# RWKV-7 recurrence in a two-layer decoder: order of values, transposes and final norms, and buffers of the sample states

## Chip, cores, metric

The kernel runs on one core of one Trainium2 chip. The metric is the device time of one execution in microseconds (us): 2224.28 us before the change, the median of three runs (2219.95 to 2230.23). The engines are named TensorE (PE; its weight loads PEld), VectorE (DVE), ScalarE (ACT), GpSimd (POOL) and SyncE (SP, which issues the DMAs here).

## The reference

One inference step of a trunk with two layers, in float32, width 1024. A prompt of 1024 rows with 16 learned rows ahead of it, and 8 samples of 8 rows each, go through the same weights: 1104 rows in all. Layer 0 is a gated DeltaNet. Layer 1 is RWKV-7 with 16 heads of width 64; the change touches only its recurrence, what stands around it, and the final norm. Cut to that:

```python
def rwkv_mixer(xn, S0, shift_prev, ...):
    r, k, v, z = ...                       # four projections of the token-shifted input
    decay = jnp.exp(-jnp.exp(w)); b_h = kk * a_h
    def step(S, inp):
        S = S * d_t + (S @ -kk_t) outer b_t + v_t outer k_t
        return S, S @ r_t                  # per head, 64 x 64 state
    S, y = lax.scan(step, S0, ...)
    y = (y - mean) * lax.rsqrt(var + GN_EPS) * lnx_w + lnx_b      # group norm per head
    y = y + jnp.sum(r_h * k_h * r_k, -1, keepdims=True) * v_h     # "bonus"
    y = y.reshape(B, T, D) * jax.nn.silu(z)
    return y @ w_o, S, xn[:, -1]
...
x = x + out
y = rmsnorm(x, final_norm_w)               # after the last layer
```

The outputs are the normed rows of the prompt and of the samples, and the states of both layers for both.

## The kernel before

The rows lie on the free axis, in three segments of 384, 384 and 336 (the first holds the 64 sample rows, chunk 0). The scan is done in chunks of 64 rows in matrix form. An *item* n = 8 s + p is one pair of heads p in one segment s: 24 items of 6 chunks each. The function `wave` runs them in *turns*: item n starts at turn T = 2 n and does one chunk a turn, so three items are in flight in each turn, and two turns start one new item. The turns run from -2 to 51, with a tail after them.

One turn on TensorE: `step_solve` (xX and rA from the state rS and AR), half of an item's *scores* (fG), `step_inner` (rA from X and rTT), `step_values` (xX of the next turn from UV and G), `step_state` (rA from UV with BT and G), and then the *dense part*: matmuls that don't hang on the recurrence, the gates (zz) till turn 14, then the output projection of segments 0, 1 and 2 (zo, at the end fo). The chain through a turn: xX goes to X on ScalarE, X through TensorE to UV on ScalarE, UV through TensorE to rS on VectorE and y on ScalarE, and rS to the next turn's xX.

All other work of an item is put at a turn, a phase of it (0 ahead of `step_solve`; 1 behind it; 1.5, 2 and 3 behind `step_state`, where 2 and 3 share the dense part between them) and a number that sorts it within the phase: `put(turn, phase, function, number)`. Each engine works through its own queue in the order in which the program is written; nothing is reordered later. The pieces that the text speaks of, by tile:

- load: DMAs of fldcs, fldr, fldv, BK, AR, rTT for an item. exps: fDp on ScalarE and DC on GpSimd. reads: AR on VectorE. pair and halves: pr on VectorE, prh on ScalarE, prl on GpSimd.
- bonus: two matmuls fbonus from prh and prl, then rbv on VectorE. values: three transposes fVT, then two copies to UV on ScalarE.
- stats and `rwkv_finish`: group norm of y (batch-norm statistics and a root on VectorE, grs on GpSimd, the scaling of y on GpSimd, for the items 22 and 23 on ScalarE with gnb), the transposes of y (dyT), their evacuation t, the gate, and the split in two float32r halves yh (ScalarE) and yl (GpSimd).
- `rwkv_sample_read`: for the 8 items of segment 0 the sample states are loaded (sn, four DMAs), transposed (dsn), copied to Sb and read. `rwkv_sample_write` brings them back (sso).
- `project_out` streams the weights of the output projection: wraw (two buffers), whi by a cast on ScalarE, wlo by a subtraction on GpSimd, as everywhere in this kernel.
- `finish(s)`: the final norm of a segment in three tiles of 128 rows: transposes (dfin, ffin, rfin), a square with a sum on ScalarE into f2k, a product with the weight on VectorE (L2073), the sum fr and its root frs, a scaling of f2k (GpSimd in the segments 0 and 1, VectorE in segment 2) and the output DMA from f2k. `fill` hands out its steps evenly over turns 31 to 45 (segment 0) and 47 to 51.5 (segment 1).

PSUM tiles have a bank by their first letter: "d" has one buffer, "f" two, "z" one, "r" three, "x" one. A new tile waits till the one before it in the same buffer has been read.

Of the kernel before, what the change touches and what calls it, by code (L numbers as in the profile page):

```python
# [11 lines left out]
ALU = mybir.AluOpType  # L12
# [13 lines left out]
class Gaps:  # L26
# [3 lines left out]
    def put(self, g, f, prio=2):  # L30
        self.q.setdefault(max(g, self.now), []).append((prio, f))
# [57 lines left out]
class Builder:  # L89
# [1604 lines left out]
    def rwkv_item(self, n, put):  # L1694

        nc, t, col = self.nc, self.t, self.pcol
        P = Ctx()
# [3 lines left out]
        T = 2 * n  # L1701
# [217 lines left out]
    def rwkv_finish(self, P, a, b):  # L1919
# [13 lines left out]
        if P.n > 21:  # L1933
            nb = t(ap, [128, 6], "gnb", 1)[:, 0:m]
            nc.vector.scalar_tensor_tensor(nb, mv[:, a:b, 0], -1.0, rs, op0=ALU.mult, op1=ALU.mult)
        for q in range(a, b):
            if P.n > 21:
                self.act(y[:, q], y[:, q], AF.Identity, scale=P.rs[:, q:q + 1], bias=nb[:, q - a:q - a + 1])
            else:
                nc.gpsimd.tensor_scalar(y[:, q], y[:, q], mv[:, q, 0:1], P.rs[:, q:q + 1], op0=ALU.subtract, op1=ALU.mult)  # L1940
# [23 lines left out]
    def rwkv_sample_read(self, P):  # L1964
# [13 lines left out]
        nc.scalar.copy(P.Sb.rearrange("p b k -> p (b k)"), sp)
# [76 lines left out]
    def finish(self, s, x2):  # L2055
# [3 lines left out]
        for q in range(3):  # L2059
# [24 lines left out]
            for h in (0, 1):  # L2084
                hs = slice(512 * h, 512 * h + 512)
                v = y[h]
                if s < 2:
                    nc.gpsimd.tensor_scalar(v[0:nr], v[0:nr], rs[0:nr], None, op0=ALU.mult)
                else:
                    nc.vector.scalar_tensor_tensor(v[0:nr], ps[h][0:nr], rs[0:nr], self.fw[0:nr, hs], op0=ALU.mult, op1=ALU.mult)  # L2090
# [436 lines left out]
    def wave(self, zin, stay, last, pool):  # L2527
# [127 lines left out]
```

## Time and profile before

| what | value |
|---|---|
| device time, median of three runs | 2224.28 us |
| profiled execution | 2241.65 us |
| its span, first to last instruction | 2239.9 us |
| mean granted clock of TensorE | 0.972 of full speed |
| busy TensorE | 2093.9 us, 93% of the span |
| busy VectorE | 1430.2 us, 64% |
| busy ScalarE | 1261.5 us, 56% |
| busy GpSimd | 1261.8 us, 56% |

The recurrence runs from about 1800 us to the end. A row of the timeline has the start, the duration, the engine, the line, the operation with output and inputs, shapes and the count of instructions that were drawn together; in brackets behind it stands how long the engine had waited before the row and for which instruction. A group of waits has three numbers: us in all, times, the longest. A row of a window has the busy time of each engine, with the count of instructions, the granted clock (1.00 is full speed), and the DMA engines' share.

### The profile page before, as it was taken

The page shows a single profiled execution, that of the slowest core. Times are in us where ns is not written, and L with a number is a line of the kernel's source. Part 1 is how long each engine was busy: PE and PEld are TensorE (multiplying, and loading weights), DVE is VectorE, ACT ScalarE, POOL GpSimd, SP SyncE. Part 2 cuts the span into 40 slices and gives each one's busy share as a digit, 9 for nine tenths or more (in the row PEclk, how much of TensorE's full clock was granted, in tenths as well). Part 3 has the DMA queues.
Part 4 walks back from the last instruction along what each step waited for, and adds up shares of the span by engine and source line. Part 5 has one row for each costly group of instructions (what it writes and reads, how often), then busy time and mean ns, then how long its engine had stood idle before and what let it go on. Part 6 is the DMA issues. An engine that isn't in the chain of part 4 may idle for free. (4 is left out here: it accounts for less than half of the span.)

```text
span 2239.9 us, 56232 instructions
## 1 busy us (share of the span) xinstructions
PE 2093.9 (93%) x20958; PEld 1955.0 (87%) x20958; DVE 1430.2 (64%) x3638; ACT 1261.5 (56%) x3627; POOL 1261.8 (56%) x1902
## 2 busy tenths in 40 slices
PE   8889999999999999989999999998989988998886
PEld 7879989899999989878998999998989977887876
DVE  7857585766757585975435762768647246776654
ACT  5526565556656565645433564756546456776653
POOL 3417768585858585525241451347668636676674
PEclk9989999999999999999999999999999989999997
DMA  4324242424343332436254235586885566755532
GB/s 119 85 58 125 65 125 73 108 80 114 86 116 95 98 108 75 131 79 177 89 148 100 68 111 173 190 253 186 239 231 146 152 172 163 200 160 153 159 116 80
DMA packets 510763, 291.67 MB, mean 130 GB/s; under 512 B 240777, under 2 KB 495866, under 8 KB 510490
## 3 DMA queue, kind: packets, MB, share of 16 engines
q1 hardware_dynamic: 510490, 288.08, 46.2%
q8 instruction: 166, 2.72, 0.5%
q14 instruction: 107, 0.88, 0.1%
HBM read 195.66 MB, written 92.30 MB: 129 GB/s over the span
## 5 line engine op out<-in xcount | busy, mean ns | idle before, releaser
L143 POOL TENSOR_TENSOR wlo<-wraw,whi 128x512 fp32r<-128x512 f32 x190 | 250.1, 1318 | 238.1 <-ACT whi L139 211.3
L692 POOL TENSOR_TENSOR invT<-invT,invtmp 72x31 f32<-72x31 f32 (+36 forms) x341 | 214.4, 629 | 26.7
L634 DVE SCALAR_TENSOR_TENSOR cvy<-raw,cw,cvy 128x408 f32<-128x408 f32 (+2 forms) x288 | 200.4, 696 | 34.2 <-ACT cvy L115 30.3
L690 POOL TENSOR_TENSOR invtmp<-invA,invT 72x31 f32<-72x31 f32 (+36 forms) x341 | 204.2, 599 | 24.8 <-DMA invA<-rltd 5.0
L129 PE MATMUL d<-xc,whi 128*128 128x384 f32 (+1 forms) x640 | 177.0, 342 | 0.0
L139 ACT CAST whi<-wraw 128x512 fp32r<-128x512 f32 x238 | 146.0, 615 | 24.4 <-DMA wraw<-in_rwkv_w_rkvz 8.5
L129 PE MATMUL dv<-xc,whi 128*128 128x384 f32 (+1 forms) x480 | 154.3, 342 | 0.0
L129 PE MATMUL dz<-xc,whi 128*128 128x384 f32 (+1 forms) x480 | 152.8, 341 | 0.0
L115 ACT ACTIVATE w<-rA,nbp 128x128 f32<-128x128 f32 x144 | 45.3, 364 | 152.8 <-PE rA L129 137.7
L129 PEld LDWEIGHTS d<-xc,whi 128*128 128x128 f32 x640 | 117.7, 191 | 1.9
L1940 POOL TENSOR_SCALAR y<-y,mv,grs 128x64 f32<-128x64 f32 x132 | 83.3, 649 | 57.8 <-DVE grs L164 34.4
L129 PE MATMUL d<-xc,wlo 128*128 128x384 f32 (+1 forms) x320 | 105.0, 338 | 2.1 <-DVE wlo L143 2.1
L160 POOL TENSOR_TENSOR ors<-ovar,cvals 128x6 f32<-128x6 f32 x24 | 34.1, 1422 | 124.6 <-DVE ovar L1122 124.6
L129 PE MATMUL dz<-xa,whi 128*128 128x384 f32 (+1 forms) x288 | 102.5, 356 | 0.5 <-DVE zg L906 0.5
L129 PE MATMUL dv<-xa,whi 128*128 128x384 f32 (+1 forms) x288 | 102.5, 356 | 0.0
L129 PE MATMUL d<-xa,whi 128*128 128x384 f32 (+1 forms) x336 | 96.3, 339 | 2.2 <-ACT whi L139 1.2
L959 POOL TENSOR_SCALAR Sb<-Sb,eglb 128x128 f32<-128x128 f32 x128 | 89.3, 710 | 6.5 <-DMA Sb<-in_state_gdn 5.1
L129 PEld LDWEIGHTS dv<-xc,whi 128*128 128x128 f32 x480 | 89.2, 188 | 3.5 <-issue 3.0
L129 PEld LDWEIGHTS dz<-xc,whi 128*128 128x128 f32 x480 | 90.2, 191 | 0.7 <-issue 0.2
L129 PE MATMUL d<-xh,whi 128*128 128x384 f32 (+1 forms) x256 | 82.7, 335 | 0.0
L129 PE MATMUL d<-xl,whi 128*128 128x384 f32 (+1 forms) x256 | 82.4, 335 | 0.0
L129 PE MATMUL d<-xh,wlo 128*128 128x384 f32 (+1 forms) x256 | 82.4, 335 | 0.0
(557 smaller groups left out, 7327.5 us busy)
## 6 DMA issues: line engine op xcount, KB each, us to landing
wraw<-in_gdn_w_in SPq DMA_DIRECT2D x96, 256.0 KB
wraw<-in_rwkv_w_rkvz SPq DMA_DIRECT2D x74, 256.0 KB
Sb<-in_state_gdn SPq DMA_DIRECT2D x64, 256.0 KB
wraw<-in_rwkv_w_o SPq DMA_DIRECT2D x48, 256.0 KB
E<-drow SPq DMA_DIRECT2D x24, 384.0 KB
attn<-drow SPq DMA_DIRECT2D x24, 384.0 KB
wraw<-in_gdn_w_out SPq DMA_DIRECT2D x36, 256.0 KB
out_s_gdn<-Sb SPq DMA_DIRECT2D x32, 256.0 KB
```

The lines of the kernel that those rows point to most:

```text
L115: return self.nc.scalar.activation(out, in_, func, bias=bias, scale=scale, **kw)
L129: self.nc.tensor.matmul(out, lhsT, rhs, start=start, stop=stop)
L139: nc.scalar.copy(hi, x)
L143: e.tensor_tensor(lo, x, hi.bitcast(F32), op=ALU.subtract)
L160: self.nc.gpsimd.tensor_tensor(y, x, half.broadcast_to(sh), op=ALU.pow)
L634: nc.vector.scalar_tensor_tensor(ys[s][:, 0:wd(s)], raws[s][:, k:k + wd(s)], cw[k], ys[s][:, 0:wd(s)], op0=ALU.mult, op1=ALU.add)
L690: v.tensor_tensor(tmp, A[:, j, j + 1:32].unsqueeze(2).broadcast_to([nb, n, m]), Tv[:, j, 0:m].unsqueeze(1).broadcast_to([nb, n, m]), op=AL ...
L692: v.tensor_tensor(Tv[:, j + 1:32, 0:m], Tv[:, j + 1:32, 0:m], tmp, op=ALU.subtract)
L959: nc.gpsimd.tensor_scalar(Sb[g][:, u], Sb[g][:, u], self.eglb[:, hv, 4 * g + u:4 * g + u + 1], None, op0=ALU.mult)
L1940: nc.gpsimd.tensor_scalar(y[:, q], y[:, q], mv[:, q, 0:1], P.rs[:, q:q + 1], op0=ALU.subtract, op1=ALU.mult)
```

## The change

- Loads and exponentials: fldcs is loaded at T - 5 instead of T - 4, the exponentials move from the end of turn T - 4 (number 6) to its phase 2 (number 2).
- Values go ahead of the dense part (2.05, where the dense part has 2.5), the bonus to the front of phase 2 (-1).
- Sample states: sn gets two buffers, Sb four, and from item 2 on the load stands at T - 5 instead of T - 4.
- y's transposes (for items up to 21) leave phase 0 of turn T + 8 and go behind the scores of that turn (phase 1); for items 20 and 21 this and what follows come a turn earlier. The steps of the items 22 and 23 are spread differently: gnb gets a second buffer, and a step of its own between it and y's scaling.
- The final norm writes to the four buffers of Sb instead of three f2k; its steps for the segments 0 and 1 stand at fixed turns (31 to 43 and 47 to 50), ahead of the dense part's first half or at the end of a turn. Segment 1's scaling moves from GpSimd to VectorE.
- The output projection of segment 2 is handed out over turns 47 to 50 and 50 to 51.8 instead of 47 to 51 and 51 to 52.

```diff
-        put(T - 4, 0, lambda: load("cs", "r"), 0)
+        put(*((T - 5, 1) if n else (-4, 0)), lambda: load("cs"), 0)
+        put(T - 4, 0, lambda: load("r"), 0.1)
...
-        put(*((T - 4, 3) if n else (-3, 1)), exps, 6)
+        put(*((T - 4, 2) if n else (-3, 1)), exps, 2)
...
-        put(T - 2, 2, values, 3)
-        put(T - 2, 2, bonus, 2)
+        put(T - 2, 2, values, 2.05)
+        put(T - 2, 2, bonus, -1)
...
-            put(T - 4, 3, go, 5)
+            put(*((T - 5, 3) if n > 1 else (-4, 3)), go, 5)
...
-            at = [(T + 5, 3, 0), (T + 6, 2, 0), (T + 8, 0, 3), (T + 8, 2, 3.4), (T + 8, 3, 2.5)]
+            e = T + 8 - (n > 19)
+            at = [(T + 5, 3, 0), (T + 6, 2, 0), (e, 1, 5.5), (e, 2, 3.4), (e, 3, 2.5)]
...
-            nb = t(ap, [128, 6], "gnb", 1)[:, 0:m]
+            nb = t(ap, [128, 6], "gnb", 2)[:, 0:m]
             nc.vector.scalar_tensor_tensor(nb, mv[:, a:b, 0], -1.0, rs, op0=ALU.mult, op1=ALU.mult)
+            yield
...
-        sn = t(self.fin, [128, 4, 2, 64], "sn", 1)
+        sn = t(self.fin, [128, 4, 2, 64], "sn", 2)
...
-        P.Sb = t(self.fin, [128, 8, 64], "Sb", 3)
+        P.Sb = t(self.fin, [128, 8, 64], "Sb", 4)
...
-                y.append(t(self.fin2, [128, 512], "f2k", 3))
+                y.append(t(self.fin, [128, 8, 64], "Sb", 4).rearrange("p b k -> p (b k)"))
...
-                    nc.gpsimd.tensor_scalar(v[0:nr], v[0:nr], rs[0:nr], None, op0=ALU.mult)
+                    (nc.vector if s else nc.gpsimd).tensor_scalar(v[0:nr], v[0:nr], rs[0:nr], None, op0=ALU.mult)
...
-        jobs += [(lambda: out(2, 0, 4, Z, ZF), 16, 47, 51), (lambda: out(2, 4, 6, Z, ZF), 8, 51, 52)]
-        more = [(lambda: self.finish(0, X2[0]), 12, 31, 45), (lambda: self.finish(1, X2[1]), 12, 47, 51.5)]
+        jobs += [(lambda: out(2, 0, 4, Z, ZF), 16, 47, 50), (lambda: out(2, 4, 6, Z, ZF), 8, 50, 51.8)]
+        more = [({31: 1, 33: 1, 34: 1, 35: 2, 37: 1, 38: 1, 39: 2, 41: 1, 42: 1, 43: 1}, 0),
+                ({47: 2, 47.5: 1, 48: 3, 48.5: 1, 49: 3, 49.5: 1, 50: 1}, 1)]
...
+        for steps, s in more:
+            for u, k in steps.items():
+                put(*((int(u), 2, lambda s=s, k=k: norm(s, k), 2.45) if u == int(u) else (int(u), 3, lambda s=s, k=k: norm(s, k), 5)))
```

How this moves the instructions, in the order of the program. First ScalarE from the end of turn 22's state step (the copies of y) to the X of turn 23 (before):

```order
L1913 COPY y_27072<-rA_27073 128x64
L139 CAST whi_27166<-wraw_26873 128x512
L1788 COPY UV_4024_23658<-fVT_27179 64x3x128 x2
L115 ACTIVATE pre_27186<-rS_3947_23066,DC_25985 128x64
L115 ACTIVATE pre_27188<-rS_3948_23067,DC_26299 128x64
L115 ACTIVATE pre_27190<-rS_3949_23068,DC_26609 128x64
L139 CAST yh_27199<-lz_26720 128x384
L115 ACTIVATE fDp_27203<-fldcs_27041 128x384
L115 ACTIVATE X_27208<-xX_27112,rk_6_84 128x64
```

The same stretch after the change:

```order
L1916 COPY y_27057<-rA_27058 128x64
L115 ACTIVATE fDp_27166<-fldcs_26931 128x384
L1788 COPY UV_4025_23660<-fVT_27170 64x3x128 x2
L139 CAST whi_27176<-wraw_26883 128x512
L115 ACTIVATE pre_27190<-rS_3947_23066,DC_25966 128x64
L115 ACTIVATE pre_27192<-rS_3948_23067,DC_26261 128x64
L115 ACTIVATE pre_27194<-rS_3949_23068,DC_26571 128x64
L139 CAST yh_27203<-lz_26722 128x384
L115 ACTIVATE X_27208<-xX_27112,rk_6_84 128x64
```

The exponential fDp moved from just ahead of X to the front of the stretch, and the copies to UV, which need the transposes fVT, stand ahead of the weight cast whi.

TensorE in the same turn, behind the state step, before:

```order
L129 MATMUL fbonus_27162<-prh_27037,bones_23062 128x384
L129 MATMUL fbonus_27162<-prl_27038,bones_23062 128x384
L129 MATMUL zo_27172<-yh_25047,whi_26869 128x384
L129 MATMUL zo_27172<-yl_25048,whi_26869 128x384
L129 MATMUL zo_27172<-yh_25047,wlo_26870 128x384
L129 MATMUL zo_27172<-yh_25366,whi_26869 128x384
L129 MATMUL zo_27172<-yl_25367,whi_26869 128x384
L129 MATMUL zo_27172<-yh_25366,wlo_26870 128x384
L126 MATMUL fVT_27179<-ident_63,fldv_26848 128x128 x3
```

And after:

```order
L129 MATMUL fbonus_27138<-prh_27039,bones_23062 128x384
L129 MATMUL fbonus_27138<-prl_27040,bones_23062 128x384
L126 MATMUL fVT_27170<-ident_63,fldv_26853 128x128 x3
L129 MATMUL zo_27182<-yh_25057,whi_26879 128x384
L129 MATMUL zo_27182<-yl_25058,whi_26879 128x384
```

The transposes fVT moved from behind six dense matmuls to right behind the bonus.

GpSimd around turn 43, where the last tile of segment 0's final norm is scaled, before:

```order
L160 TENSOR_TENSOR frs_30276<-fr_30275,cvals_68 128x1
L143 TENSOR_TENSOR wlo_30364<-wraw_30051,whi_30363 128x512
L160 TENSOR_TENSOR grs_29591<-va_29590,cvals_68 128x6
L143 TENSOR_TENSOR prl_30409<-pr_30406,prh_30408 128x384
L2088 TENSOR_SCALAR f2k_29958<-f2k_29958,frs_30276 128x512
L2088 TENSOR_SCALAR f2k_30097<-f2k_30097,frs_30276 128x512
L1940 TENSOR_SCALAR y_29506<-y_29506,mv_29589,grs_29591 128x64 x6
```

And after:

```order
L160 TENSOR_TENSOR frs_30240<-fr_30239,cvals_68 128x1
L143 TENSOR_TENSOR wlo_30246<-wraw_29933,whi_30245 128x512
L143 TENSOR_TENSOR yl_30273<-lz_29773,yh_30272 128x336
L2092 TENSOR_SCALAR Sb_29740<-Sb_29740,frs_30240 128x512
L2092 TENSOR_SCALAR Sb_30050<-Sb_30050,frs_30240 128x512
L143 TENSOR_TENSOR wlo_30371<-wraw_30061,whi_30370 128x512
L160 TENSOR_TENSOR grs_29596<-va_29595,cvals_68 128x6
L143 TENSOR_TENSOR prl_30416<-pr_30413,prh_30415 128x384
```

The two scalings moved from behind prl to ahead of one wlo, of grs and of prl. So it is in turn 39; in turn 35 they stood ahead of wlo, grs and prl before the change as well.

More of the change, by code (lines that the diff above doesn't have):

```diff
@@ L1832, in rwkv_item @@
             f = self.rwkv_finish(P, 0, 6)
-            at = [(T + 5, 3, 0), (T + 6, 2, 0), (T + 8, 0, 3), (T + 8, 2, 3.4), (T + 8, 3, 2.5)]
-            plans = [(f, at + [(T + 8, 3, 5)] * (s == 2))]
+            e = T + 8 - (n > 19)
+            at = [(T + 5, 3, 0), (T + 6, 2, 0), (e, 1, 5.5), (e, 2, 3.4), (e, 3, 2.5)]
+            plans = [(f, at + [(e, 3, 5)] * (s == 2))]
         elif n == 22:
-            plans = [(self.rwkv_finish(P, 0, 6), [(T + 5, 3, 0), (T + 6, 2, 0.5), (T + 7, 0, 2.9), (T + 7, 0, 2.95),
-                                                     (T + 7, 2, 0.5), (T + 7, 3, 5)])]
-        else:
-            plans = [(self.rwkv_finish(P, 0, 4), [(T + 3, 3, 0.1), (T + 4, 2, 0.6), (T + 5, 0, 3), (T + 5, 0, 3.1), (T + 5, 2, 0.6)]),
-                     (self.rwkv_finish(P, 4, 6), [(T + 6, 0, 2), (T + 6, 1, 2), (T + 6, 2, 2), (T + 6, 2, 2.1), (T + 6, 3, 2),
-                                                     (T + 6, 4, 2)])]
+            plans = [(self.rwkv_finish(P, 0, 6), [(T + 5, 3, 0), (T + 6, 0, 4), (T + 6, 3, 0), (T + 7, 1, 5.5), (T + 7, 1, 5.55),
+                                                  (T + 7, 2, 0.6), (T + 7, 3, 5)])]
+        else:
+            plans = [(self.rwkv_finish(P, 0, 4), [(T + 3, 3, 0.1), (T + 4, 0, 4.1), (T + 4, 3, 0.1), (T + 5, 1, 5.6), (T + 5, 1, 5.65),
+                                                  (T + 5, 2, 0.8)]),
+                     (self.rwkv_finish(P, 4, 6), [(T + 6, 0, 2), (T + 6, 1, 2), (T + 6, 1, 2.1), (T + 6, 2, 2),
+                                                  (T + 6, 2, 2.1), (T + 6, 3, 2), (T + 6, 4, 2)])]
         for f, at in plans:
@@ L2549, in wave, with fill @@
         jobs += [(lambda s=s, a=a: out(s, a, a + 4, Z), 16, 15 + 16 * s + 2 * a, 23 + 16 * s + 2 * a) for s in (0, 1) for a in (0, 4)]
-        jobs += [(lambda: out(2, 0, 4, Z, ZF), 16, 47, 51), (lambda: out(2, 4, 6, Z, ZF), 8, 51, 52)]
-        more = [(lambda: self.finish(0, X2[0]), 12, 31, 45), (lambda: self.finish(1, X2[1]), 12, 47, 51.5)]
+        jobs += [(lambda: out(2, 0, 4, Z, ZF), 16, 47, 50), (lambda: out(2, 4, 6, Z, ZF), 8, 50, 51.8)]
+        more = [({31: 1, 33: 1, 34: 1, 35: 2, 37: 1, 38: 1, 39: 2, 41: 1, 42: 1, 43: 1}, 0),
+                ({47: 2, 47.5: 1, 48: 3, 48.5: 1, 49: 3, 49.5: 1, 50: 1}, 1)]
         runs = {}
-        def fill(now, *lists):
-            for jl in lists or (jobs,):
+        def fill(now):
+            for jl in (jobs,):
                 while jl:
@@ L2580, in emit, with norm @@
                 f()
+        def norm(s, k):
+            if s not in finals:
+                finals[s] = self.finish(s, X2[s])
+            for _ in range(k):
+                next(finals[s], None)
+        finals = {}
+        for steps, s in more:
+            for u, k in steps.items():
+                put(*((int(u), 2, lambda s=s, k=k: norm(s, k), 2.45) if u == int(u) else (int(u), 3, lambda s=s, k=k: norm(s, k), 5)))
         at = lambda tau: [(P[n], tau - 2 * n) for n in range(max(0, (tau - 4) // 2), min(24, tau // 2 + 1)) if 0 <= tau - 2 * n < 6]
@@ L2600, in wave @@
             put(tau, 3, lambda: fill(tau + 1), 1)
-            put(tau, 3, lambda: fill(tau + 1, more), 7)
             emit(tau, 3)
```

## The prediction

> **What bounds the kernel now.** I read the busy shares first, then the stages, then TensorE's waits, then the engines' queues in the turns where it waits. The page's first part:
>
> ```profile
> PE 2093.9 (93%) x20958; PEld 1955.0 (87%) x20958; DVE 1430.2 (64%) x3638; ACT 1261.5 (56%) x3627; POOL 1261.8 (56%) x1902
> ```
>
> TensorE is busy 93% of the span, so a change of order can win only what it idles, plus what the clock loses by it. The change touches the recurrence and the loads just ahead of it, the last 450 us. Its stages, core 0, with the granted clock in the column PEclk:
>
> ```profile
> core 0: us, PE busy (x) PEld busy (x) DVE busy (x) ACT busy (x) POOL busy (x), PEclk, DMA share, GB/s
> 1812.00:1818.00 6.00, 5.85 (x57) 4.91 (x53) 3.27 (x8) 2.25 (x7) 3.13 (x3) 0.58 0.51 124
> 1818.00:1915.00 97.00, 85.36 (x1716) 72.58 (x1716) 64.52 (x207) 65.60 (x212) 56.36 (x68) 1.00 0.65 163
> 1915.00:2031.00 116.00, 107.43 (x2094) 96.78 (x2092) 87.90 (x283) 84.94 (x278) 82.02 (x104) 1.00 0.65 174
> 2031.00:2150.00 119.00, 104.43 (x1942) 95.45 (x1938) 82.26 (x277) 80.81 (x269) 81.94 (x99) 0.97 0.54 149
> 2150.00:2200.00 50.00, 35.29 (x422) 32.10 (x421) 24.21 (x77) 22.91 (x73) 32.11 (x35) 0.86 0.35 109
> 2200.00:2240.00 40.00, 26.15 (x174) 24.38 (x172) 17.95 (x46) 8.37 (x22) 13.63 (x13) 0.76 0.23 77
> ```
>
> These are the turns with sample states (to 1915), the plain turns (to 2031), those with the final norms of segments 0 and 1, and the end. TensorE has 11.6 us free in 97, 8.6 in 116, 14.6 in 119, 14.7 in 50 and 13.9 in 40. The other four engines stay at 76% or less in each stage. What ended TensorE's waits (in all, times, longest), from 1790 on; then two rows of 1916 to 2031 and 2031 to 2150 for the first group, and the f2k row of the latter window:
>
> ```profile
> PE rA L133 <- ACT X L115: 21.9, 24, 7.2
> PE dyT L129 <- DVE f2k L2073: 11.4, 5, 3.1
> PE dsn L126 <- DMA sn<-in_state_rwkv: 8.1, 4, 4.9
> PE fG L129 <- DVE rbv L1753: 4.3, 6, 1.6
> PE fo L129 <- POOL wlo L143: 2.4, 1, 2.4
> PE dyT L129 <- ACT Sb L1978: 2.3, 3, 0.8
> PE ffin L126 <- DVE x L2037: 1.8, 1, 1.8
> PE dfin L126 <- ACT so L1961: 1.4, 1, 1.4
> ...
> PE rA L133 <- ACT X L115: 7.0, 9, 0.8
> PE rA L133 <- ACT X L115: 5.3, 8, 1.0
> PE dyT L129 <- DVE f2k L2073: 7.9, 3, 3.1
> ```
>
> Each of these groups is touched by an edit, so the sum goes group by group.
>
> **Sample states (two buffers for sn, loads a turn earlier).** The transposes dsn wait 8.1 us for a load that could not be issued before the last head's transposes had freed the only buffer. With two buffers and, from head 2 on, the load at T-5, a load has about two turns. Bounds 0 and 8.1; I take 8.1, since nothing else holds the buffer. The four DMAs stay four on SP; for head 1 they now stand ahead of the weight loads, before the recurrence. The 4.9 us wait is also followed by the row at clock 0.58: 5.85 us of TensorE work that at full clock is up to 2.5 us shorter; I take 1.3. Sum 9.4. What is late next: the loads behind sn on SP, which have the same distance to their users as before.
>
> **y's transposes (dyT) behind the scores.** They waited 2.3 us for the PSUM bank "d", which ScalarE was still copying Sb from. Behind the scores that copy is over: 2.3. The work itself moves from ahead of xX to behind fG, so TensorE does the same sum; the state update on VectorE gets the t evacuation in front of it, while TensorE runs the inner matmuls.
>
> **The bonus ahead on VectorE (rbv).** fG waits 4.3 us in six places for rbv to empty a bank "f". It now follows rS directly, ahead of three gn and six batch-norm operations. I take 4.3. Behind it, GpSimd's scaling of y starts that much later; its y is used two turns on.
>
> **Values and exponentials ahead.** Every odd turn waits for X. Turns 22 and 23, ScalarE first, then TensorE:
>
> ```profile
> 1973.13 0.96 ACT L1788 COPY UV<-fVT 64x384 f32<-64x384 f32 x2 [1.19 <-PE fVT L126]
> 1975.13 0.52 ACT L115 ACTIVATE fDp<-fldcs 128x384 f32<-128x384 f32 x1
> 1975.68 0.73 ACT L115 ACTIVATE X<-xX,rk 128x64 f32<-128x64 f32 x3
> 1969.31 0.62 PE L133 MATMUL rA<-X,rTT 128*64 128x64 f32 x11
> 1976.05 0.80 PE L133 MATMUL rA<-X,rTT 128*64 128x64 f32 x11 [0.72 <-ACT X L115]
> ```
>
> ScalarE idles 1.19 us for the transposes fVT, which stand in the middle of the dense part, and does pre, yh and the exponential fDp (0.52) before X. With fVT ahead of the dense part and fDp in front of them, the idle 1.19 shrinks to the length of fVT and holds fDp: X starts about 0.5 to 1.1 us earlier, against a wait of 0.72. The even turn (1969.31, no idle) has none to lose. Of 7.0 + 5.3 us I take 11.0; the last turns, which have no exponential, keep the rest. Bounds 0 and 12.3.
>
> **Final norms of segments 0 and 1 at fixed places.** dfin took bank "d" at the end of a turn and held up dyT until f2k was scaled out: 7.9 us in 2031 to 2150; dfin itself waited 1.4 for so. Now dfin stands at the start of an odd turn's dense part and dyT a turn later: 9.3 gained. The price is on GpSimd, where the scaling of segment 0's rows moves ahead of prl, which the next turn's first matmul (fbonus) needs. In turn 35 it stood there before as well; in turns 39 and 43 it stood behind prl. Turn 34's prl and its user, then turn 35's scaling, prl, dyT and user:
>
> ```profile
> 2055.55 1.00 POOL L143 TENSOR_TENSOR prl<-pr,prh 128x384 fp32r<-128x384 f32 x1 [0.31 <-ACT prh L139]
> 2057.97 0.34 PE L129 MATMUL fbonus<-prl,bones 128*128 128x384 f32 x1
> 2064.74 3.30 POOL L2088 TENSOR_SCALAR f2k<-f2k,frs 128x512 f32<-128x512 f32 x2
> 2070.73 1.00 POOL L143 TENSOR_TENSOR prl<-pr,prh 128x384 fp32r<-128x384 f32 x1
> 2070.38 0.74 PE L129 MATMUL dyT<-ident,y 64*64 64x64 f32 x18 [2.42 <-DVE f2k L2073]
> 2074.29 0.34 PE L129 MATMUL fbonus<-prl,bones 128*128 128x384 f32 x1
> ```
>
> Without a scaling prl ended at 2056.55 and was needed at 2057.97, 1.4 us to spare beside an idle of 0.31, against 3.30 inserted: up to 1.6 of wait. With one (turn 35) prl ended at 2071.73; its user, which came at 2074.29 behind dyT's wait of 2.42, would have come at 2071.87: none. I take the middle, 0.8, in turns 39 and 43: 1.6; bounds 0 and 3.3 each, the whole scaling. Squares and products of dfin now stand ahead of AR and pr on VectorE: 0.2 us on X in five or so turns, an estimate, 1.0. Net 9.3 - 1.6 - 1.0 = 6.7.
>
> A rule that speaks against this place. VectorE's AR next to GpSimd's wlo:
>
> ```profile
> L1738 DVE TENSOR_TENSOR AR<-fldr,fDp x15: 526/1055/1062, 1923.8 to 2129.6; 128x384 f32<-128x384 f32 x15
> 1966.07 1.06 DVE L1738 TENSOR_TENSOR AR<-fldr,fDp 128x384 f32<-128x384 f32 x1
> 1965.43 1.29 POOL L143 TENSOR_TENSOR wlo<-wraw,whi 128x512 fp32r<-128x512 f32 x1 [0.82 <-ACT whi L139]
> ```
>
> AR takes 0.53 at best, 1.06 mostly, and here ends 0.41 after wlo does: it seems to stand still while GpSimd works. The Trainium skill ("SBUF — State Buffer", "SBUF: two separate sides") says that VectorE, when it reads two SBUF tensors, and GpSimd lock a port pair against each other for a whole instruction; the trace agrees with its 1.06. By that rule each scaling, 3.30 / 2 = 1.65 long, would hold AR up longer than wlo's 1.29 does; the sum by it is among the rivals.
>
> **The end.** Segment 1's norm and the last norms had three buffers f2k; now four Sb buffers, free by then. Rows picked out of ScalarE, TensorE, ScalarE and VectorE (the last two at the very end), then GpSimd, TensorE and ScalarE around turn 47:
>
> ```profile
> 2174.01 0.60 ACT L115 ACTIVATE f2k<-ffin 128x512 f32<-128x512 f32 x1 [6.47 <-DMA out_y_prompt<-f2k]
> 2174.96 0.79 PE L133 MATMUL rA<-X,rTT 128*64 128x64 f32 x7 [7.18 <-ACT X L115]
> 2232.89 0.59 ACT L115 ACTIVATE f2k<-rfin 80x512 f32<-80x512 f32 x1 [3.17 <-DMA out_y_prompt<-f2k]
> 2233.61 0.16 DVE L2078 TENSOR_TENSOR fr<-fr 80x1 f32<-80x1 f32 x1 [2.23 <-ACT f2k L115]
> 2149.44 2.92 POOL L1940 TENSOR_SCALAR y<-y,mv,grs 128x64 f32<-128x64 f32 x5
> 2151.22 0.79 PE L133 MATMUL rA<-X,rTT 128*64 128x64 f32 x11 [0.59 <-ACT X L115]
> 2156.16 0.62 ACT L139 CAST whi<-wraw 128x512 fp32r<-128x512 f32 x1 [1.72 <-DMA wraw<-in_rwkv_w_o]
> ```
>
> A square waits 6.47 us for an output DMA to free its buffer, X stands behind it, and TensorE idles 7.18: gone with the fourth buffer and VectorE scaling instead of GpSimd. Its half clock: (1 - 0.86) x 35.29 = 4.9 at most in that stage, I take 1.0. The same wait at 2232.89 (3.17) holds the last norm: VectorE's fr stands idle 2.23 for it at 2233.61, so 2.2 off the end, uncovered by anything. dyT for f2k: 11.4 - 7.9 = 3.5. ffin 1.8 (x behind gnb, which gets a second buffer and earlier roots). fo for wlo 2.4 (the scalings leave GpSimd). Sum 7.2 + 1.0 + 2.2 + 3.5 + 1.8 + 2.4 = 18.1.
> Prices. Item 20's dyT comes a turn earlier, at turn 47: its y is ready at 2149.44 + 2.92 = 2152.36, dyT takes about 0.7, so rA starts at 2153.1 instead of 2151.22, of which 0.7 is moved work: 1.2. The output projection of segment 2 runs 8 tiles in 3 turns instead of 4, and its casts stand in front of X on ScalarE: a weight still landing cost 1.72 at 2156.16 (off the path); I take two such on the path, 3.4. wlo may be late again as before: 2.4. Net 18.1 - 7.0 = 11.1; bounds 4 and 22 (no price, full clock).
>
> **Sum.** 9.4 + 2.3 + 4.3 + 11.0 + 6.7 + 11.1 = 44.8. Waits that go let the next in line show; I take back a quarter, 11, most of it in the sample turns and at the end, where waits stand among queues of two thirds' load (ScalarE 65.60, VectorE 64.52 of 97). Gain 33.8. The profiled execution took 2241.65 us, 1.75 more than its span of 2239.9; less 33.8 it is 2207.9. The median of the three runs, 2224.28, is 17.4 below the profiled one, which is slower all through; from the median the forecast is 2190.
>
> **The rivals.** First, the waits move on: SP's loads, GpSimd's prl and ScalarE's casts become the bound in the sample turns, the norm turns and the end, and of 44.8 a third stays: 2224.3 - 15 = 2209. For it: DMA is at 0.65 in the sample turns; against it: VectorE, ScalarE and GpSimd are below 70% there.
> Second, the port: segment 0's scaling stops AR, pr, prh and with them prl and X by one scaling more, 1.65 us in turns 39 and 43, 3.3: 2193. For it is AR's 1.06; against it that AR stands still for wlo already.
> Third, nothing changes: the listed waits hide others of the same size that end just after. For it: X, rbv and sn end within a microsecond of each other in some turns; against it: 7.18 and 3.17 have one cause each. 2224, within 11 us.
> Fourth, slower: the chain X, UV, state, next X sets the turn and not TensorE. Then dyT, 0.74 us at 2070.38, now between fG and rA, lengthens 22 turns, and the waits freed elsewhere return at X: 22 x 0.74 = 16, 2240. It decides if X is ready when fG ends and yet rA, delayed by dyT, delays the next turn. Against it: the even turns, where dyT goes, show no idle at 1969.31, and the dense part lies between rS and the next xX.
>
> **Chances.** The forecast (gain of 22 and more) 0.54, the moved waits 0.22, the port 0.10, nothing 0.08, slower 0.06. 0.5%, 11 us, is about what a measurement of this kernel tells from no change. Faster takes the forecast, the port and four fifths of the moved waits, 0.82; same 0.12; slower 0.06. The range: all waits gone and no price is 61 us (9.4 + 1.2 + 2.3 + 4.3 + 12.3 + 9.3 + 22), 2163, which I don't expect; 54 of them give 2170. At the other end the moved waits with a little less, a gain of 9: 2215.
>
> **What would show it.** Right: dsn without a wait for sn; no fG waiting for rbv, no dyT for f2k; odd turns' rA without X; no idle of several us near turn 49; the last squares back to back; row 1812 to 1818's clock near 1. Wrong: fbonus waiting for prl in turns 39 and 43 by more than 2 us, X behind whi casts at the end, TensorE idle beyond 40 us from 1800 on, or even turns longer by dyT.

## The result, and the profile after

The changed kernel takes 2201.14 us (median of four runs, 2195.32 to 2203.38), the one before 2227.26 (four runs, 2219.95 to 2231.66): a ratio of 0.9882, 95% interval 0.9847 to 0.9917. It is 26 us (1.2%) faster; the forecast was 34 us, to 2190. The profiled execution took 2200.14 us, 41.5 less than that of before. But 20.6 of these 41.5 lie ahead of the first gate matmul (zz at 1792.0 us before, at 1771.4 after), in layer 0 and the dense part. That start lies between 1771 and 1792 us in the fourteen profiles of this study, at 1775 to 1792 in five with the old recurrence and at 1771 to 1783 in nine with the new; two profiles of the changed kernel alone differ there by 12 us (1771.4 and 1783.3), so it says little of the edits. So the stages are measured from landmarks, that is, from events that every kernel has: the first gate matmul, and the start of X on ScalarE in turns 0, 8, 18, 30, 46 and 51. The changed kernel, in these stages:

```profile
PE 2083.4 (95%) x20958; PEld 1945.7 (89%) x20958; DVE 1434.5 (65%) x3644; ACT 1260.2 (57%) x3627; POOL 1253.1 (57%) x1896
```

```profile
1771.40:1787.00 15.60, 14.07 (x150) 12.84 (x147) 4.39 (x10) 6.85 (x15) 6.25 (x8) 0.82 0.77 225
1787.00:1836.40 49.40, 46.27 (x866) 39.36 (x866) 34.02 (x103) 34.35 (x109) 25.13 (x31) 1.00 0.68 177
1836.40:1920.00 83.60, 72.60 (x1321) 62.48 (x1323) 55.42 (x176) 50.40 (x167) 52.75 (x63) 0.90 0.62 162
1920.00:1998.90 78.90, 78.76 (x1532) 72.66 (x1528) 64.08 (x199) 60.60 (x200) 56.77 (x72) 1.00 0.63 174
1998.90:2118.40 119.50, 111.04 (x2007) 101.72 (x2005) 85.57 (x283) 84.47 (x279) 87.80 (x104) 0.96 0.56 157
2118.40:2167.70 49.30, 40.14 (x483) 36.03 (x481) 31.18 (x97) 25.48 (x83) 29.57 (x34) 0.97 0.44 140
2167.70:2198.40 30.70, 21.71 (x200) 20.02 (x194) 15.61 (x46) 8.57 (x25) 8.19 (x10) 0.81 0.21 66
```

And two of the same stages before, turns 8 to 18 and 18 to 30:

```profile
1867.80:1941.80 74.00, 64.51 (x1308) 55.27 (x1303) 55.15 (x177) 50.92 (x165) 51.83 (x62) 1.00 0.69 177
1941.80:2022.70 80.90, 76.22 (x1516) 69.69 (x1510) 60.99 (x199) 60.19 (x199) 56.81 (x72) 1.00 0.63 168
```

All stages of all kernels, in us. A name with a_ is the changed kernel with an edit, with b_ the kernel before with one; the experiments below tell which, and after_again is the changed kernel once more. Where two kernels have the same order in a stage, they mostly agree within 0.3 us. Turns 0 to 8, and turn 8 with the load of BK, vary by a few us, and two other stages by 1.3 (turns 9 to 17, 71.7 in after and 70.4 in a_projection_late; turns 46 to 51, 49.3 in after and 50.6 in a_scale_vector). Each stage is one profile of one execution.

| kernel | zz to 0 | 0-8 | 8-18 | 18-30 | 30-46 | 46-51 | 51-end | sum |
|---|---|---|---|---|---|---|---|---|
| before | 20.8 | 55.0 | 74.0 | 80.9 | 122.7 | 50.8 | 43.7 | 447.9 |
| after | 15.6 | 49.4 | 83.5 | 78.9 | 119.5 | 49.3 | 30.7 | 427.0 |
| after_again | 15.5 | 48.8 | 83.6 | 78.9 | 119.5 | 49.3 | 30.8 | 426.4 |
| b_sn | 15.2 | 57.7 | 77.1 | 80.9 | 122.6 | 50.9 | 43.7 | 448.0 |
| b_values | 21.0 | 60.7 | 71.6 | 75.5 | 124.2 | 51.1 | 43.7 | 447.8 |
| b_bonus_ahead | 22.0 | 57.9 | 81.0 | 80.9 | 123.9 | 51.9 | 43.0 | 460.5 |
| b_four_buffers | 20.5 | 54.7 | 73.3 | 80.9 | 125.9 | 45.8 | 42.0 | 442.9 |
| a_bonus_behind | 15.8 | 50.8 | 71.5 | 79.0 | 119.8 | 49.4 | 31.0 | 417.3 |
| a_dyT_first | 15.6 | 51.0 | 80.3 | 78.7 | 117.5 | 49.1 | 30.4 | 422.5 |
| a_scale_vector | 15.4 | 51.0 | 80.6 | 79.0 | 114.9 | 50.6 | 30.1 | 421.6 |
| a_projection_late | 15.5 | 49.2 | 80.1 | 79.0 | 119.5 | 37.8 | 37.6 | 418.6 |
| a_best | 16.1 | 52.4 | 71.7 | 79.2 | 115.2 | 50.2 | 30.2 | 414.9 |
| a_best2 | 16.2 | 51.7 | 75.0 | 79.0 | 115.4 | 38.0 | 37.2 | 412.4 |
| a_best3 | 15.7 | 51.3 | 71.2 | 79.0 | 113.2 | 38.5 | 36.7 | 405.5 |

From the first gate matmul to the end the kernel gained 20.9 us: 5.2 and 5.6 up to turn 8, and 14.5 from turn 46 on. In the 280 us between, where 24 us were forecast (dyT, rbv, values, norms, ahead of the quarter taken back), the gain is -9.5 + 2.0 + 3.2 = -4.3. TensorE's waits from 1790 us on (us, times, longest):

```profile
PE rA L133 <- ACT X L115: 13.7, 15, 2.6
PE fbonus L129 <- DMA wraw<-in_rwkv_w_o: 3.8, 2, 2.1
PE zo L129 <- DVE x L2041: 3.0, 1, 3.0
PE fG L129 <- DMA BK<-kpd: 2.0, 1, 2.0
PE fbonus L129 <- POOL prl L143: 1.7, 1, 1.7
PE fo L129 <- POOL wlo L143: 1.0, 1, 1.0
```

The groups "dyT for f2k", "dsn for sn" and "fG for rbv" of before are gone, as forecast. X is still waited for, 7.1 of the 13.7 in turns 8 to 18, where it was 1.9 before; and fbonus waits for prl three times (1.7, 1.7 and 2.1 us; two of these the list puts down to a DMA, which is taken up below).

### The profile page after: what moved, and what is told of

It is laid out like the page before. It is cut to its first block, busy times and chain, and to the rows that moved or that the text cites. A ratio compares the mean times of both kernels' runs of the same rounds, so it can differ in the third digit from the quotient of the medians.

```text
span 2198.4 us, 56220 instructions
## 1 busy us (share of the span) xinstructions
PE 2083.4 (95%) x20958; PEld 1945.7 (89%) x20958; DVE 1434.5 (65%) x3644; ACT 1260.2 (57%) x3627; POOL 1253.1 (57%) x1896
```

## The experiments

**Turns 8 to 18: the bonus ahead.** In one sample turn of the changed kernel, VectorE, then ScalarE, then TensorE:

```profile
1860.10 0.56 DVE L1753 TENSOR_TENSOR rbv<-fldv,fbonus 128x384 f32<-128x384 f32 x1 [1.04 <-PE fbonus L129]
...
1862.06 0.65 DVE L2006 TENSOR_TENSOR Sb<-Sb,drsw 128x512 f32<-128x512 f32 x1
1862.75 0.69 DVE L2007 TENSOR_TENSOR Sb<-Sb,DC 128x512 f32<-128x512 f32 x1
1863.36 0.62 DVE L1954 SCALAR_TENSOR_TENSOR lz<-t,lnb,lz 128x384 f32<-128x384 f32 x1
1864.01 0.51 ACT L139 CAST yh<-lz 128x384 fp32r<-128x384 f32 x1 [2.13 <-DVE lz L1954]
1864.55 0.72 ACT L115 ACTIVATE X<-xX,rk 128x64 f32<-128x64 f32 x3
1864.91 0.80 PE L133 MATMUL rA<-X,rTT 128*64 128x64 f32 x11 [1.03 <-ACT X L115]
```

VectorE stands still 1.04 us for fbonus, with rbv first in its queue; roots, statistics, two steps on Sb and lz wait behind it. ScalarE waits 2.13 for lz, with yh ahead of X, and TensorE 1.03 for X. Then the clock (the third column from the right in rows of 0.75 us):

```profile
1863.25:1864.00 0.75, 0.63 (x22) 1.00 0.72 207
1864.00:1864.75 0.75, 0.00 (x0) 1.00 1.06 238
1864.75:1865.50 0.75, 0.59 (x12) 1.00 1.00 223
1865.50:1866.25 0.75, 0.75 (x23) 0.68 0.95 272
1866.25:1867.00 0.75, 0.75 (x20) 0.50 1.17 286
...
1868.50:1869.25 0.75, 0.75 (x4) 0.54 0.00 0
1869.25:1870.00 0.75, 0.75 (x9) 1.00 0.00 0
```

Soon after the wait TensorE runs 3.4 us at half clock. Three edits were put against each other, and the changed kernel was run once more.

```diff
# a_bonus_behind
-        put(T - 2, 2, bonus, -1)
+        put(T - 2, 2, bonus, 2 if n < 10 else -1)
```

> The changed kernel, with the bonus of the items 0 to 9 back behind the group-norm roots and statistics (number 2). The turns 8 to 18 (start of X to start of X) took 74.0 us before the change and 83.5 after. Theory A (rbv, first in VectorE's queue, waits for fbonus there, and statistics, Sb, lz, then yh and X on ScalarE all come later): 75 to 79 us, yh's wait for lz below 0.8 each, no half-clock stretch in turns 9 to 17, the whole 4 to 8 us shorter. Theory B (dyT behind the scores makes lz late): 82 to 85, no gain. Theory C (the load of BK that came 2.0 late, and chance): 81 to 85.

```diff
# a_dyT_first
-            at = [(T + 5, 3, 0), (T + 6, 2, 0), (e, 1, 5.5), (e, 2, 3.4), (e, 3, 2.5)]
+            at = [(T + 5, 3, 0), (T + 6, 2, 0), (e, 0, 3) if n < 20 else (e, 1, 5.5), (e, 2, 3.4), (e, 3, 2.5)]
```

> The changed kernel, with y's transposes dyT of the items 0 to 19 back in phase 0, ahead of xX. Theory A (standing alone between fG and rA, dyT takes TensorE 0.35 us more a turn pair than when it overlaps xX): turns 18 to 30 take 76.8 us instead of 78.9, turns 8 to 18 stay within 2 of 83.5, the whole is 2 to 5 us shorter. Theory B (dyT makes lz late in the sample turns): turns 8 to 18 take 78 or less. Rival: the place costs nothing and the waits for bank d come back: turns 18 to 30 take 79 to 80, the whole is 0 to 4 longer.

```diff
# b_bonus_ahead: the kernel before
-        put(T - 2, 2, bonus, 2)
+        put(T - 2, 2, bonus, -1)
```

> The kernel before with the bonus at the front of phase 2, nothing else. If rbv's place alone makes lz and X late in the sample turns: turns 8 to 18 in 78 to 82 us instead of 74.0; if it does so only together with dyT behind the scores: 72 to 75. Turns 18 to 30 stay at 80.9 within 0.3, since fG waits for rbv there once in no turn pair of them.

after_again, the changed kernel once more:

> The changed kernel once more, on the chip of a_best. If the loss in turns 8 to 18 lies in the order of instructions, they take 80 to 84 us again, the stages from 18 on agree with the first profile within 1 us each; if it was chance, they take 72 to 77.

a_bonus_behind took 71.5 us there, less than theory A had said and less than before the change; after_again took 83.6, and from turn 18 on it agrees with the first profile within 0.1 us in each stage. So the loss in turns 9 to 17 is not chance: 71.7 us in both profiles of the changed kernel, 62.7 in a_bonus_behind. Turn 8 is another matter. It took 11.9 us in both, behind a wait of 2.0 and 2.1 us for the load of BK with half clock after it; with the same order there it took 9.7 in a_scale_vector and a_projection_late, and with the bonus behind it took 8.8 in a_bonus_behind, 7.7 in a_best and 10.9 in a_best2. So of the 12.0 us between after and a_bonus_behind 8.9 lie in turns 9 to 17 and belong to the bonus; for the 3.1 of turn 8, theory C's load of BK stays open.

Waits of yh on ScalarE and of rA on TensorE in turns 8 to 18 (changed kernel, then a_bonus_behind with its stage, then b_bonus_ahead):

```profile
ACT yh L139 <- DVE lz L1954: 9.1, 5, 2.1
PE rA L133 <- ACT X L115: 7.1, 5, 2.6
```

```profile
ACT yh L139 <- DVE lz L1954: 3.7, 5, 1.0
PE rA L133 <- ACT X L115: 0.8, 2, 0.4
1847.00:1918.50 71.50, 65.82 (x1321) 56.46 (x1323) 54.81 (x176) 50.70 (x166) 52.79 (x62) 1.00 0.73 189
```

```profile
ACT yh L139 <- DVE lz L1950: 7.0, 5, 2.1
PE rA L133 <- ACT X L115: 8.7, 5, 3.0
```

The waits of yh fell from 9.1 to 3.7 (one of 1.0 is more than the 0.8 that was expected), X's from 7.1 to 0.8, and the clock is 1.00. fG's wait for rbv came back (2.9 us), and the stage is shorter all the same. b_bonus_ahead shows the same from the other side, with dyT where it was: 81.0 us for 74.0, of which 5.8 lie in turns 9 to 17, with yh's waits at 7.0 (1.6 before) and X's at 8.7 (1.9 before). That is theory A: rbv's place alone is enough. With dyT first turns 8 to 18 still take 80.3 us: the loss stays, and the 3.3 are turn 8 alone (8.2 us for 11.9). The timed medians: a_bonus_behind 2201.0 us (ratio to before 0.986, 0.9823 to 0.9896), a_dyT_first 2205.5 (0.9879), b_bonus_ahead 2251.1 in one run against 2226.7. Beside the changed kernel's 0.9882 and 0.9892 the timed medians of a_bonus_behind and a_dyT_first tell no difference; the stages do.

**Turns 18 to 30: where the gain of values and exponentials went.** a_dyT_first had 78.7 us there, not the 76.8 of theory A: in its even turns dyT does overlap xX again, and the 0.35 us that this gives are then waited for X (1.6 us in five turns). The waits of dyT for the bank "d" came back too (1.5 us for Sb, ahead of turn 18). So as long as X is this late, dyT's place costs and gives nothing there. The values alone show more:

```diff
# b_values: the kernel before
-        put(T - 4, 0, lambda: load("cs", "r"), 0)
+        put(*((T - 5, 1) if n else (-4, 0)), lambda: load("cs"), 0)
+        put(T - 4, 0, lambda: load("r"), 0.1)
-        put(*((T - 4, 3) if n else (-3, 1)), exps, 6)
+        put(*((T - 4, 2) if n else (-3, 1)), exps, 2)
-        put(T - 2, 2, values, 3)
+        put(T - 2, 2, values, 2.05)
```

> The kernel before with values, exponentials and the load of fldcs moved as in the change, nothing else. Theory (the whole gain in the plain turns is X's, and what dyT's place costs there it gives back as cover for X): turns 18 to 30 in 78.6 to 79.2 us (80.9 before, 78.9 after, 78.7 with dyT first). Rival (it needs the bonus ahead or dyT behind): 80 or more.

75.5 us: 5.4 less than before, below the range of my theory, and 3.2 below a_dyT_first, from which it differs in these turns by nothing but the bonus's place, on VectorE rbv's (on TensorE both have fbonus, fVT, zo in this order). VectorE's AR in turns 18 to 30 (count, then shortest, median and longest in ns), a_dyT_first and then b_values:

```profile
L1738 DVE TENSOR_TENSOR AR<-fldr,fDp x6: 1685/1738/1740, 1933.3 to 1998.9; 128x384 f32<-128x384 f32 x6
1959.61 1.69 DVE L1738 TENSOR_TENSOR AR<-fldr,fDp 128x384 f32<-128x384 f32 x1
1959.60 1.28 POOL L143 TENSOR_TENSOR wlo<-wraw,whi 128x512 fp32r<-128x512 f32 x1
1962.39 0.51 ACT L139 CAST prh<-pr 128x384 fp32r<-128x384 f32 x1 [0.83 <-DVE pr L1742]
```

```profile
L1738 DVE TENSOR_TENSOR AR<-fldr,fDp x6: 1131/1154/1173, 1945.9 to 2008.9; 128x384 f32<-128x384 f32 x6
1971.13 1.13 DVE L1738 TENSOR_TENSOR AR<-fldr,fDp 128x384 f32<-128x384 f32 x1
1970.55 1.30 POOL L143 TENSOR_TENSOR wlo<-wraw,whi 128x512 fp32r<-128x512 f32 x1
1973.41 0.52 ACT L139 CAST prh<-pr 128x384 fp32r<-128x384 f32 x1 [0.31 <-DVE pr L1742]
```

With rbv ahead, the roots come half a microsecond later, so does GpSimd's scaling of y, and the wlo behind it then starts together with AR instead of 0.58 ahead of it. AR ends 0.41 to 0.42 after wlo in both. Held up so, AR takes 1.7 us for 1.15, and ScalarE waits 0.83 for pr instead of 0.31 ahead of prh, behind which X stands. In a_dyT_first rA then waits 0.31 us for X in such a turn, in b_values not at all. So with the values ahead and dyT first, the bonus's place costs the plain turns 3.2 us. With the values in their old place it costs nothing there (b_bonus_ahead 80.9, as before and as expected). In the changed kernel dyT fills the time in which X is late, and the trace lists no wait; what the bonus costs there was not measured, for the bonus was not put behind in all turns.

**Sample states.**

```diff
# b_sn: the kernel before
-        sn = t(self.fin, [128, 4, 2, 64], "sn", 1)
+        sn = t(self.fin, [128, 4, 2, 64], "sn", 2)
-            put(T - 4, 3, go, 5)
+            put(*((T - 5, 3) if n > 1 else (-4, 3)), go, 5)
```

> The kernel before with two buffers for sn and its load at T - 5 from item 2 on, nothing else. Theory (the gain at the start is the load): from the first gate matmul to X of turn 0 15.5 to 16.5 us instead of 20.8, turns 0 to 8 in 51 to 53 instead of 55.0, turns 8 to 18 in 71 to 74 (74.0). Rival: turns 0 to 8 gained by the values and the bonus: they stay at 54 to 55.

The start fell to 15.2 us as expected, but turns 0 to 18 took 5.8 us more, and nothing is left (448.0). ScalarE, then TensorE at the end of turn 6 of b_sn:

```profile
1843.83 0.52 ACT L115 ACTIVATE fDp<-fldcs 128x384 f32<-128x384 f32 x1 [3.96 <-DMA fldcs<-csd]
1844.74 1.01 PE L133 MATMUL rA<-X,rTT 128*64 128x64 f32 x11 [2.62 <-ACT X L115]
```

ScalarE waits 3.96 us for fldcs, for the exponential, and X stands behind that. Both rival and theory missed it. The other way round b_values, which loads fldcs a turn earlier, waits 8.1 us for sn in turns 0 to 8 and takes 60.7 us there. The changed kernel has both edits, waits for neither, and gains 10.8 us up to turn 8; no run has these two without the others.

**Turns 30 to 46: the norms of segment 0.** GpSimd in turn 39 of the changed kernel, then TensorE, then VectorE beside the scaling:

```profile
2069.74 3.51 POOL L2092 TENSOR_SCALAR Sb<-Sb,frs 128x512 f32<-128x512 f32 x2 [0.51 <-DVE frs L164]
2075.77 0.99 POOL L143 TENSOR_TENSOR prl<-pr,prh 128x384 fp32r<-128x384 f32 x1
2076.82 0.44 PE L129 MATMUL fbonus<-prl,bones 128*128 128x384 f32 x1 [1.72 <-DMA wraw<-in_rwkv_w_o]
2070.16 0.67 DVE L1738 TENSOR_TENSOR AR<-fldr,fDp 128x384 f32<-128x384 f32 x1
```

```diff
# a_scale_vector
-                    (nc.vector if s else nc.gpsimd).tensor_scalar(v[0:nr], v[0:nr], rs[0:nr], None, op0=ALU.mult)
+                    nc.vector.tensor_scalar(v[0:nr], v[0:nr], rs[0:nr], None, op0=ALU.mult)
```

> The changed kernel, with segment 0's final scaling on VectorE too. Theory A: the three waits of fbonus for prl (1.7, 1.7, 2.1 us) go, since GpSimd is rid of 3.4 us in each of three turns, and VectorE pays about 1.0 each; turns 30 to 46 take 114 to 116 us instead of 119.5, the whole is 4 to 6 shorter. Rival: the waits are for the weight load that the trace names, or VectorE hands the time on to pr and rS: 118 to 120.

114.9 us, as theory A said, and no wait of fbonus. (The wait of 1.72 is put down to a DMA, but prl ends at 2076.76, right at its end.) In their place come three waits of fG in the turns 35, 39 and 43 (2.0, 2.0 and 1.6 us), for which the trace names no cause. The timed median is 2205.5 (0.9884, 0.9842 to 0.9927), within the noise. What it gained in turns 32, 36, 40 and 44 (10.6 us, the sum of 7.3, 8.0, 9.5 and 10.0 less that of 6.0, 6.0, 6.1 and 6.1) it paid back in part in 35, 39 and 43, each 2.0 to 2.1 longer; that is the rival's second half, VectorE handing time on. VectorE and GpSimd in turn 39 of a_scale_vector:

```profile
2074.03 1.83 DVE L162 TENSOR_TENSOR fn_t<-frs 128x1 f32<-128x1 f32 x1
2077.68 0.55 DVE L1738 TENSOR_TENSOR AR<-fldr,fDp 128x384 f32<-128x384 f32 x1
2073.59 1.00 POOL L143 TENSOR_TENSOR yl<-lz,yh 128x384 fp32r<-128x384 f32 x1
2074.55 1.28 POOL L143 TENSOR_TENSOR wlo<-wraw,whi 128x512 fp32r<-128x512 f32 x1
```

fn_t, 0.15 to 0.16 us long in the kernel before, stood still till GpSimd's wlo had ended at 2075.83 (in turns 35 and 43 it took 1.89 and 1.66). AR, behind it in the queue, ends at 2078.23, and fG, which reads AR, starts at 2078.33 after its wait of 1.97.

**The end.**

```diff
# b_four_buffers: the kernel before
-                y.append(t(self.fin2, [128, 512], "f2k", 3))
+                y.append(t(self.fin2, [128, 512], "f2k", 4))
```

> The kernel before, with four buffers f2k instead of three and nothing else. Theory A (the end's gain is the buffer): from X of turn 46 to the end 94.5 us before, now 82 to 86; no square waits for an output DMA longer than 1 us; the whole is 9 to 12 us shorter. Rival (the gain of 14.5 at the end comes from the other edits there: scaling on VectorE, earlier steps, gnb): 91 us or more, the whole less than 4 shorter.

```diff
# a_projection_late
-        jobs += [(lambda: out(2, 0, 4, Z, ZF), 16, 47, 50), (lambda: out(2, 4, 6, Z, ZF), 8, 50, 51.8)]
+        jobs += [(lambda: out(2, 0, 4, Z, ZF), 16, 47, 51), (lambda: out(2, 4, 6, Z, ZF), 8, 51, 52)]
```

> The changed kernel with segment 2's output projection handed out over turns 47 to 51 and 51 to 52 again. Theory (what the end gained beyond the buffer is matmuls of the projection done before turn 51): X of turn 51 to the end takes 37 to 42 us instead of 30.7, turns 46 to 51 take 45 to 48 instead of 49.3. Rival (it is the steps of the items 22 and 23 and gnb): 30 to 33 at the end.

From turn 46 on the fourth buffer alone gives 6.8 of the 14.5 us, between theory and rival; the squares' waits for output DMAs (14.0 us before) are gone, as theory A said. The buffer cost 3.2 in turns 30 to 46, and the whole is 0.9957 of the time before (0.9932 to 0.9983). The projection surprised: handed out late it takes 6.9 us more behind turn 51, as expected, but 11.5 less ahead of it, so that the earlier projection costs 4.6 (5.2 between a_best and a_best2 below). Turns 46 to 51 of a_projection_late and ScalarE's waits there, against the changed kernel's:

```profile
2118.80:2156.60 37.80, 35.56 (x487) 31.52 (x481) 27.84 (x94) 24.07 (x79) 25.03 (x30) 1.00 0.49 153
ACT whi L139 <- DMA wraw<-in_rwkv_w_o: 3.4, 3, 1.6
```

```profile
ACT whi L139 <- DMA wraw<-in_rwkv_w_o: 10.0, 3, 5.4
```

Spread over three turns the weights come too late: ScalarE waits 10.0 us for them, X behind it, and TensorE idles 9.2 us (49.30 - 40.14) instead of 2.2. The trace puts 3.0 us of this down to X, where a_projection_late has 0.9, and 3.0 to the sum of x (L2041), which reads zo; that this too comes from the weights is not shown. The other 4.6 of the 11.5 are busy time, mostly projection work that is done behind turn 51 instead.

**Together.** a_best is a_bonus_behind with a_scale_vector, a_best2 adds a_projection_late, and a_best3 moves segment 0's root and scaling, still on VectorE, to the end of the turns 35, 39 and 43, behind pr.

> The changed kernel with both edits: the bonus of the items 0 to 9 behind the statistics, and segment 0's final scaling on VectorE. If the two causes are separate, their gains add: turns 8 to 18 in 71 to 73 us (83.5 after the change), turns 30 to 46 in 114 to 116 (119.5), from the first gate matmul to the end 410 to 414 (427.0), and the whole 12 to 17 us shorter than the changed kernel, about 0.981 of the time before. Rival: the stages hand the time on to the next, 416 or more.

> a_best with segment 2's output projection handed out as before the change (47 to 51, 51 to 52). If the third cause is separate as well: turns 46 to 51 in 38 to 40 us, turn 51 to the end 36 to 38, from the first gate matmul to the end 409 to 412, the whole 3 to 6 us below a_best's 2190.6. Rival: 414 or more, no gain.

> a_best2 with segment 0's root and scaling (on VectorE) at the end of the turns 35, 39 and 43, behind pr, each tile of the norm with steps of its own. Theory (in the turns 35, 39, 43, 9.6 us instead of 7.5, VectorE's fn_t of 0.16 us stood 1.8 us still beside GpSimd's yl and wlo, which read two SBUF tensors as it does): turns 30 to 46 in 109 to 112 us instead of 115.1. Rival (behind pr it stands still beside prl and makes G late): 114 or more.

```diff
# a_best3, beside the edits above
-        more = [({31: 1, 33: 1, 34: 1, 35: 2, 37: 1, 38: 1, 39: 2, 41: 1, 42: 1, 43: 1}, 0),
+        more = [({31 + 4 * q: 1, 33 + 4 * q: 1, 34 + 4 * q: 1, 35.5 + 4 * q: 1}, q / 4) for q in range(3)]
...
-                finals[s] = self.finish(s, X2[s])
+                finals[s] = self.finish(1, X2[1]) if s == 1 else self.finish(0, X2[0], [int(4 * s)])
...
-                put(*((int(u), 2, lambda s=s, k=k: norm(s, k), 2.45) if u == int(u) else (int(u), 3, lambda s=s, k=k: norm(s, k), 5)))
+                put(*((int(u), 2, lambda s=s, k=k: norm(s, k), 2.45) if u == int(u) else (int(u), 3, lambda s=s, k=k: norm(s, k), 5 if s == 1 else 6.5)))
```

The first two causes are separate: in a_best both stages gained what they had gained alone (71.7 and 115.2), the whole from the first gate matmul is 414.9, just above the 410 to 414 expected, and the timed median is 2190.6 us (0.9825, 0.9802 to 0.9848), clear of the changed kernel on the same chip (2208.2; 0.9892, 0.9869 to 0.9916). The third shows in the stages only: a_best2 has the expected 38.0 and 37.2, but 412.4 in all, and its median of 2189.0 (0.9823, 0.9797 to 0.985) tells no gain beside a_best (in the profile, its turn 8 is 3.2 us longer than a_best's, behind a wait of 2.1 us for BK). a_best3 took 2184.6 (0.9806, 0.978 to 0.9832). In a_best3 turns 30 to 46 took 113.2, above the 109 to 112 expected though under the rival's 114: the turns 35, 39 and 43 fell to 7.7, 7.6 and 7.4, while 32, 36, 40 and 44 rose to 6.7 to 7.3, where X again is late. Its median and its profile are the shortest here, but its interval overlaps that of the two others. The runs with a single execution, b_sn, b_values and a_projection_late, took 2230.2, 2232.4 and 2195.9 us beside medians of 2232.2, 2226.7 and 2232.2 before.

## Why the prediction was right, and where not

The time lies in the range and the direction is right; the gain is three quarters of the forecast. Of the 26 us timed, the stages account for 20.9; the rest is not traced to any edit. That the time fell into the range owes something to luck, for the sum missed in both directions: up to turn 8 and from turn 46 on the stages gained 25.3 us where 9.4 + 11.1 were forecast, and between them they lost 4.3 where 24.3 were to be gained. By its steps, in the trace:

- **Sample states**, 9.4: 10.8 up to turn 8, together with the other edits. Alone (b_sn) it gained 2.9 up to turn 8 and lost as much by turn 18. About right in size; "the same distance to their users" did not keep the loads behind sn in time: fldcs came late in b_sn, BK in the changed kernel (2.0 us). The half clock after the long wait is gone as forecast.
- **dyT**, 2.3: no gain shown. Its wait for the bank did go and came back with dyT first, but its place is worth nothing in the plain turns, and with dyT first turns 30 to 46 are 2.0 shorter.
- **The bonus**, 4.3: the step that failed. fG's wait for rbv did go, but I priced what stands behind the moved instruction at nothing ("its y is used two turns on"), and VectorE's queue behind it is statistics, Sb, lz, then yh and X on ScalarE. Instead of gaining 4.3 it cost 8.9 us in turns 9 to 17 (71.7 for 62.7); in the kernel before the same edit alone cost 5.8 there. A wait moved to the front of a queue is paid by all behind it.
- **Values and exponentials**, 11.0: the mechanism is right, and in the twelve plain turns the edit alone is worth 5.4 (b_values). In the changed kernel 2.0 of it are left there: AR, held up beside wlo, makes X late again, and dyT now stands alone between fG and rA. Odd turns' rA waits for X no more there, as forecast.
- **Norms of segments 0 and 1**, 6.7: 3.2 in turns 30 to 46. The price of fbonus was mis-sized: 5.5 us in three turns (1.7, 1.7 and 2.1) where I took 1.6 in two, turn 35 included, since the row that gave "none" had the idle of dyT in it.
- **The end**, 11.1: 14.5. The buffer gave less than the 9.4 that I had ascribed to the waits for it (7.2 and 2.2), the rest of the edits more; of the prices, the weights landing late were forecast at 3.4 us and cost 4.6 net.
- **The quarter taken back**, 11, covers part of the loss by its size, not by its cause: it was meant for waits that move on, while the largest loss was made by an edit that the sum had counted as a gain.

Of the rivals, the port's clash did come about, but not as told. The scaling on GpSimd did not stop VectorE: AR beside it took 0.68 and 0.67 us in the turns 35 and 39. The trace of before had shown it already in turn 35, in the middle of the scaling that runs from 2064.74 to 2068.04:

```profile
2066.08 0.53 DVE L1738 TENSOR_TENSOR AR<-fldr,fDp 128x384 f32<-128x384 f32 x1
```

So the 1.65 us a scaling that the rival took are borne out by neither trace. What AR stands still beside is GpSimd's wlo, and the change moved wlo against AR: in the plain turns AR took 1.06 us before and 1.72 after. The Trainium skill ("SBUF — State Buffer", "SBUF: two separate sides") says that a VectorE instruction with two inputs in SBUF and a GpSimd one that reads SBUF exclude each other for a whole instruction. AR's end 0.40 to 0.43 behind wlo's in both kernels agrees; its 0.53 us inside a scaling, which reads SBUF as well, does not, and the measurement decides. "The waits move on" was right for fbonus and for the casts of whi at the end. The chain-bound rival did not show: the even turns have no wait that dyT makes. TensorE's idle time is 40.9 us from turn 0 on (the rows above from the second on, length less busy time), and 39.4 from 1800 us on: right at the 40 that I had named as a sign against.

## What to carry to other kernels

Before an instruction that waits for another engine is moved ahead in a queue, list what stands behind it, up to the next instruction that another engine waits for: here, over lz and yh, that was the chain's own X. Edits that feed the same turn must be tried one by one in both directions: sn without fldcs and fldcs without sn each left the whole as it was (448.0 and 447.8 for 447.9), and one edit of the change, the bonus, cost 9 us beside a net gain of 21. Compare stages between landmarks, not whole spans: two executions of the changed kernel differed by 12 us ahead of the recurrence, their stages from turn 8 on by at most 0.1.

## What the runs showed of the hardware

- A VectorE instruction on 128x1, 0.15 to 0.16 us long in the kernel before, stood still and took 1.83 us, through the rest of one GpSimd subtraction (yl) and the whole of the next (wlo), each of two tensors. In all fourteen profiles AR, when it overlapped a wlo, took 0.64 to 2.06 us and ended 0.40 to 0.43 behind it; beside GpSimd's scaling of one tensor it took 0.52 to 0.68 us, and 0.52 to 0.56 with nothing beside it.
- Waits of TensorE of 0.7 to 0.8 us in the plain turns before left the granted clock at 1.00, and so did a wait of 1.5 us in turn 8 of a_bonus_behind. In turns 8 to 18 of the changed kernel five stretches of 3.4 us at 0.50 came at the end of or behind single waits of 2.0 and 2.6 us, and behind waits of 0.4 us with another of 0.9, 1.0 or 1.3 us within 2.9 us; they leave these turns a mean clock of 0.90. The Trainium skill ("TensorE: Matmul & The Clock Gate", "What's actually happening") says that the clock is halved after at least one idle window of about 3.4 us and full again after at least one busy window of that length. The length of the slow stretches agrees with the second; the waits ahead of them were shorter than the first, and the measurement decides.
